# Two projections whose first call takes four column blocks, and eleven products at the start

## The chip, the cores and the metric

The kernel runs on one core of a Trainium2 chip. Its engines each work through their own row of instructions in order: TensorE (PE in the profile, with PEld for the loading of weights), VectorE (DVE), ScalarE (ACT), GpSimd (POOL), and SyncE (SP), which here issues the transfers. The metric is the device time of one execution in microseconds (us).

## The reference

One layer of an encoder: 256 rows of x, 2048 wide, 256 rows of memory. The parts that the change touches are the two projections `w_out` and `w_o`, each added to x. The attention's weights are a softmax over the memory rows for each of four heads.

```python
h = rms_norm(x, norm_mix_g[l])
x = x + hybrid_mixer(h, ...)            # ends in: merged @ w_out
h = rms_norm(x, norm_x_g[l])
mem_n = rms_norm(mem, norm_mem_g[l])
x = x + cross_attention(h, mem_n, w_xq[l], w_xkv[l], w_xo[l])
...
def cross_attention(h, mem_n, w_q, w_kv, w_o):
    q = (h @ w_q).reshape(b, s, XATTN_HEADS, XATTN_DH)
    k, v = jnp.split(mem_n @ w_kv, 2, axis=-1)
...
    p = jax.nn.softmax(scores, axis=-1)
    o = jnp.einsum("bhsm,bmhd->bshd", p, v).reshape(b, s, D_MODEL)
    return o @ w_o
```

Behind these stands an MLP with 8192 hidden columns. All inputs are float32.

## The kernel before

Every large product streams a weight matrix from memory once. `fetch` (L74 to L98) brings 1 MB of it at a time into a buffer `raw` of which there are three, and splits it in two halves: for each half ACT writes the high part `whi` (L93) and DVE the rest `wlo` (L94), in three buffers each. With `rush` the 1 MB comes in two transfers of 512 KB. A product of two float32 matrices is then made of two or three products of such parts. The activations lie as such pairs too, in tiles named `q` (`Quad`).

The order of the instructions on each engine comes from a scheduler that goes by the order of the code, by data that must be there, by free buffers and by priorities; `tc.high_priority(offset=...)` moves what stands in it forward. Each engine then keeps its row and waits at each instruction until its inputs and its buffer are there.

PSUM, where TensorE writes, is given out from three rings: `s0` and `s1`, two banks each, by `stream_ps()`, and `b`, four banks, by `bank()`. The ring `b` serves the transposes in `to_feature` (L238), the attention's scores (`sps`), its transposed weights (`tps`), its outputs (`ops`), and more.

There are two ways to stream a matrix. `chunk` (L134 to L136) makes 512 columns for 2 row tiles at a time, three products each. `blocks` (L158 to L180) makes `nb` blocks of 128 columns: for each of the 16 row blocks `nb` products with `whi` (L172, 512 wide) and `nb` with `wlo` (L174, 256 wide). One fetch holds 16 / `nb` row blocks. At the end ACT (L178) and DVE (L179) take each block out of its bank into a tile `bo`, of which there are two, and `evac` goes on with it.

Three places matter here.

The start: the first `chunk` is that of the values (`w_xkv`, `values(0)`). Its `before` loads 512 columns of the memory rows (`xc`, `load_mem`), transposes them on TensorE against `ident` (L238), and ACT (L251) and DVE (L252) write them into `q`, scaled by `gains`. ACT also sums squares of those rows (`junk`, L266). `ident` is made by POOL at L207, and the gains come through a transpose of 16 rows (`grow`, L224).

`w_out`: the last `chunk` of the mixer's gates (`w_in`, columns from `C_TB`) ends in `evac` of `sig_gate` (ACT L802 writes `gth`, DVE L814 and L816 write `yg`), then `to_feature` transposes `yg` into the last quad of `merged`. The call `residual_pass(merged, w_out[0], G_X, "n2", load_x)` follows: eight calls of `blocks` with two column blocks each, each with its 256 columns of x through `loader`.

`w_xo`: for each head the attention makes the scores (L104 to L106, 24 products into `sps`), their maximum (DVE L929, L930), the exponentials (ACT L934), the scaled weights `pr` (DVE L936, L938), four transposes of these into `tps` (L943), their parts `pth` and `ptl` (ACT L100, DVE L101), and the outputs (L104 to L106 again, from `pth`, `ptl`, `vvh`, `vvl`). After the last head comes `residual_pass(att, w_xo[0], G_FFN, "n3")`, which needs all heads for its 16 row blocks but takes the first twelve from the earlier heads. The scheduler lays products of it between the instructions of the last head.

Of the kernel before, what the change touches and what calls it, by code (L numbers as in the profile page):

```python
# [17 lines left out]
P = 128  # L18
# [32 lines left out]
def trunk(ctx: ExitStack, tc: tile.TileContext, x, mem, positions, norm_mix_g, w_in, conv_w, gdn_a_log, gdn_dt_bias,  # L51
# [4 lines left out]
    act, vec, pool, pe = nc.scalar, nc.vector, nc.gpsimd, nc.tensor  # L56
# [9 lines left out]
    def stream_ps():  # L66
        s0 = psp.tile([P, 512], F32, name="s0", tag="s0", bufs=2)
        s1 = psp.tile([P, 512], F32, name="s1", tag="s1", bufs=2)
        return s0, s1

    def bank():
        return psp.tile([P, 512], F32, name="b", tag="b", bufs=4)


    def fetch(pieces, k, n, rush=False, hold=None, at=0):

        raw = wp.tile([P, k * n], F32, name="raw", tag="raw", bufs=3)
        rv = raw.rearrange("p (k n) -> p k n", k=k)
        with tc.high_priority(offset=100000):
            for off, ap in pieces:  # L80
                src = ap.rearrange("(k p) n -> p k n", p=P)
                for ks in ((slice(0, k // 2), slice(k // 2, k)) if rush else (slice(0, k),)):
                    nc.sync.dma_start(rv[:, ks, off:off + ap.shape[1]], src[:, ks, :])
            got = []
            for i in range(2):
                if hold:
                    both = hold().both
                    hi, lo = (both[:, a:a + 2, :].rearrange("p a s -> p (a s)") for a in (0, 2))
                else:
                    hi, lo = (wp.tile([P, 1024 + ROOM], F32R, name=e, tag=e, bufs=3)[:, at:at + k * n // 2]  # L90
                              for e in ("whi", "wlo"))
                src = raw[:, i * k * n // 2:(i + 1) * k * n // 2]
                act.activation(hi, src, AF.Copy)  # L93
                vec.tensor_sub(lo, src, hi.bitcast(F32))  # L94
                got.append((hi.rearrange("p (k n) -> p k n", n=n), lo.rearrange("p (k n) -> p k n", n=n)))
        return got
# [61 lines left out]
    def blocks(quads, w, c0, nb, evac):  # L158

        k = 16 // nb
        ps = stream_ps()
        n = nb * P
        for g in range(KT // k):
            halves = fetch([(0, w[g * k * P:(g + 1) * k * P, c0:c0 + n])], k, n, at=SHIFT)
            for i in range(k):
                kk = g * k + i
                xh, xhl = quads[kk // 4][0][:, kk % 4, :], quads[kk // 4].both[:, kk % 4, :]
                wh, wl = (a[:, i % (k // 2), :] for a in halves[i // (k // 2)])  # L170
                for b in range(nb):
                    pe.matmul(ps[b], wh[:, b * P:(b + 1) * P], xhl, start=kk == 0, stop=False)  # L172
                for b in range(nb):
                    pe.matmul(ps[b][:, :S], wl[:, b * P:(b + 1) * P], xh, start=False, stop=kk == KT - 1)  # L174
        for b in range(nb):
            with tc.high_priority(offset=50000):
                o = sm.tile([P, S], F32, name="bo", tag="bo", bufs=2)
                act.activation(o, ps[b][:, S:], AF.Copy)  # L178
                vec.tensor_add(o, o, ps[b][:, :S])  # L179
                evac(b, o)  # L180
# [23 lines left out]
    ident = cp.tile([P, P], F32, name="ident")  # L204
# [7 lines left out]

    def rsqrt(o, i):
        pool.tensor_tensor(o, i, nhalf_pow[:, :o.shape[1]], op=ALU.pow)

    gains = cp.tile([P, 64], F32, name="gains")

# [37 lines left out]
    def rms_cols(name, ssq, count=D):  # L255

        s = sm.tile([P, NT], F32, name=f"{name}_s", tag="rc_s")
        vec.tensor_reduce(s, ssq, axis=AX.X, op=ALU.add)
        vec.tensor_scalar(s, s, 1.0 / count, EPS, op0=ALU.mult, op1=ALU.add)
        r = cp.tile([P, NT], F32, name=f"{name}_r")  # L260
        rsqrt(r, s)
        return r
# [67 lines left out]
    for k2 in range(8):  # L330
        ps = bank()
# [9 lines left out]
        for f in range(2):  # L341
            k = 2 * k2 + f
# [13 lines left out]
    for a in range(2):  # L356
        ps = bank()
# [156 lines left out]
    for b2 in range(8):  # L514
        ko = kv.tile([P, 2, S], F32, name="ko", tag="vo", bufs=2)

        def evac_k(b, ps):
            vec.tensor_mul(ko[:, b, :], ps, mrow)

        blocks(memq, w_xkv[0], b2 * 256, 2, evac_k)  # L520
        nc.sync.dma_start(kt_d[:, 2 * b2:2 * b2 + 2, :], ko)
        for h in ((0,), (2, 4), (6, 8), (10,), (12,), (14,), (), ())[b2]:
            decays(h)
        if 2 <= b2 < 6:
            ret_decays(2 * b2 - 4)
# [24 lines left out]
    def gdn_stream(grp):  # L550
# [4 lines left out]
        for pr in range(2):  # L555
# [5 lines left out]
            for part, c0, bofs in ((1, C_GQ, 0), (0, C_GK, 16), (2, C_GV, 32)):  # L561
                def evac(b, ps, part=part, bofs=bofs):
                    if part < 2:
                        conv_silu(bofs + h0 + b, ps, kq[:, b, part, :])
                    else:
                        vt = mx.tile([P, S], F32, name="vt", tag="vt", bufs=2)
                        conv_silu(bofs + h0 + b, ps, vt)
                        vts.append(vt)
                blocks(h1, w_in[0], c0 + h0 * GD, 2, evac)
# [169 lines left out]
    def retention(j, yr):  # L739
        qk = mx.tile([P, 4, S], F32, name="qk", tag="qk", bufs=1)  # L740

        for a2, c0 in ((0, C_RQ), (2, C_RK)):
            def evac_qk(b, ps):

                rb = mx.tile([P, S], F32, name="rb", tag="rb", bufs=2)
                act.activation(rb[0:64], ps[64:128], AF.Copy)
                act.activation(rb[64:128], ps[0:64], AF.Copy)
                o = qk[:, a2 + b, :]
                vec.tensor_mul(o, ps, cos)
                vec.tensor_mul(rb, rb, sin)  # L750
                vec.tensor_add(o, o, rb)

            blocks(h1, w_in[0], c0 + 256 * j, 2, evac_qk)
# [104 lines left out]
    rt = tp.tile([P, KT, S], F32, name="rt", tag="rt", bufs=1)  # L858
# [3 lines left out]
    def quad_b():  # L862
        return new_quad(q2p, 4)
# [8 lines left out]
    def residual_pass(quads, w, gain, name, loader=None):  # L872
        nxt = []
        acc = xa.tile([P, S], F32, name="acc2", tag="acc2", bufs=2)
        vec.memset(acc, 0.0)
        for b2 in range(8):
            xc = loader(b2) if loader else None
            if b2 % 2 == 0:
                nxt.append(quad_b())

            def evac(b, ps):
                k = 2 * b2 + b
                vec.tensor_add(rt[:, k, :], ps, xc[:, b, :] if loader else rt[:, k, :])
                g = gains[:, gain + k:gain + k + 1]
                qh, ql = (a[:, k % 4, :] for a in nxt[-1])
                act.activation(qh, rt[:, k, :], AF.Copy, scale=g)
                vec.scalar_tensor_tensor(ql, rt[:, k, :], g, qh.bitcast(F32), op0=ALU.mult, op1=ALU.subtract)
                sq = xa.tile([P, S], F32, name="sq2", tag="sq2", bufs=2)
                act.activation(sq, rt[:, k, :], AF.Square)
                vec.tensor_add(acc, acc, sq)  # L890

            blocks(quads, w, b2 * 256, 2, evac)
        ps = bank()
        for t in range(NT):
            pe.matmul(ps[:, 2 * t:2 * t + 2], acc[:, t * P:(t + 1) * P], ones[:, :2], start=True, stop=True)
        s = sm.tile([P, NT], F32, name=f"{name}_s", tag="rc_s")
        vec.tensor_scalar(s, ps[:, 0:4:2], 1.0 / D, EPS, op0=ALU.mult, op1=ALU.add)
        r = cp.tile([P, NT], F32, name=f"{name}_r")
        rsqrt(r, s)
        return nxt, r  # L900

    def load_x(b2):
        xc = xa.tile([P, 2, S], F32, name="xc2", tag="xc2", bufs=2)
        nc.sync.dma_start(xc, xt_d[:, 2 * b2:2 * b2 + 2, :])
        return xc

    h2, rstd2 = residual_pass(merged, w_out[0], G_X, "n2", load_x)
    rstd2s = cp.tile([P, NT], F32, name="rstd2s")
    vec.tensor_scalar_mul(rstd2s, rstd2, XD ** -0.5)
# [3 lines left out]
    for h in range(XH):  # L913
# [14 lines left out]
        nb = xa.tile([P, NT], F32, name="nb", tag="nb", bufs=2)  # L928
# [27 lines left out]
        att.append(quad)  # L956

    h3, rstd3 = residual_pass(att, w_xo[0], G_FFN, "n3")
    rstd3q = cp.tile([P, NT], F32, name="rstd3q")
    vec.tensor_mul(rstd3q, rstd3, rstd3)  # L960
# [7 lines left out]
    for c in range(4):  # L968
        for t in range(NT):
            ps = bank()  # L970
# [95 lines left out]
```

## Time and profile before

| | |
|---|---|
| runs | 2086.66, 2086.51 and 2084.16 us; median 2086.51 us |
| the profiled execution | 2084.37 us |
| its span in the profile | 2082.6 us |
| instructions in the trace | 28439 |
| mean granted clock of TensorE | 0.999 |
| bytes moved | 405.09 MB, 195 GB/s |

The span runs from the first to the last event of the execution; 1.8 us lie around it. In the lists below a line has a start, a duration, the engine, the line of the kernel, the operation, what it writes and reads, how many instructions are put together in it, and in brackets how long the engine had been idle before and what ended that. PE's durations overlap, since products are pipelined: the distance of two starts is what one costs.

### The profile page before, as it was taken

To read this page: it belongs to the slowest core of one execution; us is meant where nothing else is said; L and a number is where in the kernel's file an instruction comes from. 1 tells how busy PE (TensorE), PEld (TensorE's weight loads), DVE (VectorE), ACT (ScalarE), POOL (GpSimd) and SP (SyncE) were. 2 spreads that over 40 slices of the span, in tenths; PEclk is the share of its full clock that TensorE was granted. 3 is DMA by queue.
4 is the path that set the end of the run, shared out by engine and by line. 5 is a ranking of instruction groups with operands and counts; after the bars stand their busy time and mean duration, and the time that the engine had idled before them with its cause. 6 is when DMAs were issued, how large, how long until landed. Compare 5 with 4: busy or idle time off the path is not lost.

```text
span 2082.6 us, 28439 instructions
## 1 busy us (share of the span) xinstructions
PE 2062.4 (99%) x11028; PEld 1776.8 (85%) x11028; DVE 1396.9 (67%) x2261; ACT 1081.8 (52%) x1630; POOL 31.1 (1%) x37
## 2 busy tenths in 40 slices
PE   8999999999999999999999999999999999999998
PEld 6888888888888888888888898888888888888887
DVE  6785779577966786678757665756556546645654
ACT  7554564566446644565455555554444434434444
POOL 0000000000000000000000000000000000000000
PEclk9999999999999999999999999999999999999999
DMA  8796656555555565555657654666566556556653
GB/s 292 234 315 224 202 175 211 168 182 175 199 185 165 175 200 186 171 183 172 199 183 235 193 182 142 188 196 196 189 196 188 195 189 194 190 196 188 195 189 142
DMA packets 314342, 405.09 MB, mean 195 GB/s; under 512 B 18512, under 2 KB 222304, under 8 KB 314080
## 3 DMA queue, kind: packets, MB, share of 16 engines
q1 hardware_dynamic: 314208, 403.29, 59.8%
q8 instruction: 86, 1.41, 0.3%
q14 instruction: 48, 0.39, 0.1%
HBM read 389.61 MB, written 13.65 MB: 194 GB/s over the span
## 4 chain that ended last, share of the span: by engine, by line
PE 97%; DMA 1%; SPq 1%; DVE 0%; issue 0%; ACT 0%; ACTq 0%; POOLq 0%; POOL 0%; DVEq 0%
PE s L172 34%; PE s L174 17%; PE s L135 14%; PE s L136 14%; PE s L134 14%; PE b L684 1%; PE b L587 1%; DMA xc<-x 1%; PE b L104 0%; PE b L106 0%; PE b L105 0%; SPq L285 0%; DMA vr<-vv_d 0%; PE b L589 0%; PE b L585 0%
## 5 line engine op out<-in xcount | busy, mean ns | idle before, releaser
L94 DVE TENSOR_TENSOR wlo<-raw,whi 128x1024 fp32r<-128x1024 f32 x700 | 855.4, 1223 | 575.4 <-ACT whi L93 571.7
L93 ACT ACTIVATE whi<-raw 128x1024 fp32r<-128x1024 f32 x700 | 741.4, 1060 | 814.9 <-PE s L172 378.9
L172 PE MATMUL s<-q,whi 128*128 128x512 f32 x3072 | 959.9, 393 | 3.4 <-DVE bo L179 3.2
L174 PEld LDWEIGHTS s<-q,wlo 128*128 128x128 f32 x3072 | 575.2, 188 | 123.2 <-DVE wlo L94 1.1
L174 PE MATMUL s<-q,wlo 128*128 128x256 f32 x3072 | 615.8, 280 | 0.5 <-DVE wlo L94 0.5
L135 PE MATMUL s<-wlo,q 128*128 128x512 f32 x1264 | 495.7, 392 | 0.5 <-DVE wlo L94 0.5
L136 PE MATMUL s<-whi,q 128*128 128x512 f32 x1264 | 491.8, 390 | 0.0
L172 PEld LDWEIGHTS s<-q,whi 128*128 128x128 f32 x3072 | 468.8, 188 | 7.3 <-DVE bo L179 3.6
L134 PE MATMUL s<-whi,q 128*128 128x512 f32 x1264 | 452.3, 390 | 0.0
L134 PEld LDWEIGHTS s<-whi,q 128*128 128x128 f32 x1264 | 237.7, 188 | 48.9 <-ACT q L251 0.4
L135 PEld LDWEIGHTS s<-wlo,q 128*128 128x128 f32 x1264 | 237.8, 188 | 48.3 <-DVE wlo L94 0.9
L136 PEld LDWEIGHTS s<-whi,q 128*128 128x128 f32 x1264 | 237.7, 188 | 47.4
L179 DVE TENSOR_TENSOR bo<-bo,s 128x256 f32<-128x256 f32 x192 | 72.2, 413 | 0.0
L178 ACT ACTIVATE bo<-s 128x256 f32<-128x256 f32 x192 | 62.4, 372 | 17.3 <-DVE dj L593 17.3
L536 DVE SCALAR_TENSOR_TENSOR acc<-bo,cw,acc 128x255 f32<-128x255 f32 (+2 forms) x144 | 61.8, 477 | 3.0 <-ACT acc L533 2.8
L644 DVE TENSOR_TENSOR pr<-lw,tw 32x31 f32<-32x31 f32 (+15 forms) x124 | 40.3, 325 | 10.5 <-DMA lw<-scr_l 8.7
L646 DVE TENSOR_TENSOR tw<-tw,pr 32x31 f32<-32x31 f32 (+15 forms) x124 | 40.6, 327 | 2.1
L994 DVE SCALAR_TENSOR_TENSOR res<-s,rstd3q,res 128x512 f32<-128x512 f32 (+1 forms) x32 | 22.3, 735 | 12.0 <-PE s L136 12.0
L986 DVE TENSOR_TENSOR q<-hs,q 128x256 fp32r<-128x256 f32 x64 | 24.1, 419 | 0.8 <-ACT q L985 0.8
L983 DVE SCALAR_TENSOR_TENSOR hs<-bo 128x256 f32<-128x256 f32 x64 | 24.2, 419 | 0.0
L533 ACT ACTIVATE acc<-bo,cw 128x256 f32<-128x256 f32 x48 | 22.0, 499 | 1.6 <-PE b L585 0.8
L985 ACT ACTIVATE q<-hs 128x256 fp32r<-128x256 f32 x64 | 22.7, 402 | 0.0
(313 smaller groups left out, 1041.7 us busy)
## 6 DMA issues: line engine op xcount, KB each, us to landing
raw<-w_in SPq DMA_DIRECT2D x143, 1024.0 KB, 4.9
raw<-w_ff SPq DMA_DIRECT2D x128, 1024.0 KB, 5.2
raw<-w_xkv SPq DMA_DIRECT2D x31, 1024.0 KB, 5.7
raw<-w_out SPq DMA_DIRECT2D x16, 1024.0 KB, 5.3
raw<-w_xq SPq DMA_DIRECT2D x16, 1024.0 KB, 6.1
raw<-w_xo SPq DMA_DIRECT2D x16, 1024.0 KB, 5.8
dec_d<-dec_w SPq DMA_DIRECT2D x8, 384.0 KB, 11.1
dec<-dec_d SPq DMA_DIRECT2D x8, 384.0 KB, 4.3
```

Source lines behind the costliest of these rows:

```text
L93: act.activation(hi, src, AF.Copy)
L94: vec.tensor_sub(lo, src, hi.bitcast(F32))
L134: pe.matmul(o, xh, wh, start=first, stop=False)
L135: pe.matmul(o, xh, wl, start=False, stop=False)
L136: pe.matmul(o, xl, wh, start=False, stop=last)
L172: pe.matmul(ps[b], wh[:, b * P:(b + 1) * P], xhl, start=kk == 0, stop=False)
L174: pe.matmul(ps[b][:, :S], wl[:, b * P:(b + 1) * P], xh, start=False, stop=kk == KT - 1)
L178: act.activation(o, ps[b][:, S:], AF.Copy)
L179: vec.tensor_add(o, o, ps[b][:, :S])
L536: vec.scalar_tensor_tensor(acc[:, d:], ps[:, :S - d], cw[:, j, blk:blk + 1], acc[:, d:], op0=ALU.mult, op1=ALU.add)
L644: vec.tensor_mul(pv, lw[:, j, j + 1:32].unsqueeze(2).to_broadcast([32, n, j + 1]), tw[:, j, 0:j + 1].unsqueeze(1).to_broadcast([32, n, j + ...
L646: vec.tensor_sub(tw[:, j + 1:32, 0:j + 1], tw[:, j + 1:32, 0:j + 1], pv)
```

## The change

The first call of each residual projection takes 512 columns, four blocks, where it was two calls of 256; the other six stay. The two further banks come from the ring `b`. In that call a fetch holds 4 row blocks of 512 columns instead of 8 of 256; the number of products, fetches and transfers is the same, and two tiles of x are loaded ahead of the call. At the start eleven products `ident` by `ident` are written into a bank of the ring `b`, at the highest priority in the program; nobody reads them. Lines behind the change have numbers 5 or 6 higher.

```diff
         k = 16 // nb
-        ps = stream_ps()
+        ps = stream_ps() if nb < 3 else (*stream_ps(), bank(), bank())
...
+    with tc.high_priority(offset=300000):
+        wps = bank()
+        for _ in range(11):
+            pe.matmul(wps[:, :P], ident, ident, start=True, stop=True)
...
-        for b2 in range(8):
-            xc = loader(b2) if loader else None
+        for b2 in (0, 2, 3, 4, 5, 6, 7):
+            nb = 2 if b2 else 4
+            xc = [loader(b2 + i) for i in range(nb // 2)] if loader else None
...
-                vec.tensor_add(rt[:, k, :], ps, xc[:, b, :] if loader else rt[:, k, :])
+                vec.tensor_add(rt[:, k, :], ps, xc[b // 2][:, b % 2, :] if loader else rt[:, k, :])
...
-            blocks(quads, w, b2 * 256, 2, evac)
+            blocks(quads, w, b2 * 256, nb, evac)
```

The order of the instructions differs at three places only: up to the end of the first values, around the first call of `w_out`, and around the first call of `w_xo`. Everything between and behind them stands in the same order as before.

At the start ACT's row, before the change, is this one (the first `whi` is the first half of the first 1 MB, the second `whi` its other half; `xc` are memory rows, `b` their transposes):

```order
L203 ACTIVATE warm<-warm 128x1
L93 ACTIVATE whi<-raw 128x1024
L266 ACTIVATE junk,ssqm<-xc 128x512 x2
L251 ACTIVATE q<-b,gains 128x256
L93 ACTIVATE whi<-raw 128x1024
L251 ACTIVATE q<-b,gains 128x256 x2
```

And with the change:

```order
L203 ACTIVATE warm<-warm 128x1
L93 ACTIVATE whi<-raw 128x1024 x2
L271 ACTIVATE junk,ssqm<-xc 128x512
L256 ACTIVATE q<-b,gains 128x256 x2
L271 ACTIVATE junk,ssqm<-xc 128x512
L256 ACTIVATE q<-b,gains 128x256
```

Both halves of the first piece now stand ahead of the first `q`, and one sum of squares instead of two.

On PE at `w_out`, before the change, the transposes of `yg` stand behind all 24 pairs of products of the first twelve row blocks for the first two column blocks, and one pair of L172 of the next call (here the end of these and the beginning of that call):

```order
L174 MATMUL s_10101<-q,wlo 128x256
L174 MATMUL s_10102<-q,wlo 128x256
L172 MATMUL s_10207<-q,whi 128x512
L172 MATMUL s_10208<-q,whi 128x512
L238 MATMUL b<-ident,yg 128x128 x2
L174 MATMUL s_10207<-q,wlo 128x256
L174 MATMUL s_10208<-q,wlo 128x256
L172 MATMUL s_10207<-q,whi 128x512
```

And with the change, where the four column blocks are `s_10115`, `s_10116` and two banks `b`:

```order
L172 MATMUL s_10115<-q,whi 128x512
L172 MATMUL s_10116<-q,whi 128x512
L174 MATMUL s_10115<-q,wlo 128x256
L174 MATMUL s_10116<-q,wlo 128x256
L243 MATMUL b<-ident,yg 128x128 x2
L172 MATMUL b<-q,whi 128x512 x2
L174 MATMUL b<-q,wlo 128x256 x2
L172 MATMUL b<-q,whi 128x512 x2
L174 MATMUL b<-q,wlo 128x256 x2
```

The first two transposes now stand behind the 12 pairs of six row blocks, and ahead of the 12 pairs that the same row blocks have on the two banks `b`; the other six transposes follow those.

On PE at `w_xo`, before the change, thirty products of the projection stand between the last head's scores and the transposes of its weights. These are the last of them:

```order
L172 MATMUL s_12190<-q,whi 128x512
L172 MATMUL s_12191<-q,whi 128x512
L174 MATMUL s_12190<-q,wlo 128x256
L174 MATMUL s_12191<-q,wlo 128x256
L943 MATMUL b<-ident,pr 128x128 x4
L172 MATMUL s_12190<-q,whi 128x512
L172 MATMUL s_12191<-q,whi 128x512
```

With the change the scores' last products, the transposes and the first products from `pth` stand side by side, and behind them six row blocks on one bank `b`:

```order
L104 MATMUL b<-kth,qth 128x256
L105 MATMUL b<-ktl,qth 128x256
L106 MATMUL b<-kth,qtl 128x256
L949 MATMUL b<-ident,pr 128x128 x4
L104 MATMUL b<-pth,vvh 128x256 x2
L172 MATMUL b<-q,whi 128x512
L174 MATMUL b<-q,wlo 128x256
L172 MATMUL b<-q,whi 128x512
L174 MATMUL b<-q,wlo 128x256
```

The two blocks on `s0` and `s1` have gone ahead of the scores by six row blocks, as far as the three buffers of `whi` reach, and the two blocks on `b` come where the banks of scores and weights come free.

## The prediction

> **What bounds the kernel now.** I read the page's busy times and its chain first, then the list of what PE waits for, then the timeline at the places that the change touches.
>
> ```profile
> PE 2062.4 (99%) x11028; PEld 1776.8 (85%) x11028; DVE 1396.9 (67%) x2261; ACT 1081.8 (52%) x1630; POOL 31.1 (1%) x37
> ...
> PE 97%; DMA 1%; SPq 1%; DVE 0%; issue 0%; ACT 0%; ACTq 0%; POOLq 0%; POOL 0%; DVEq 0%
> ```
>
> PE is busy for 99% of the span and carries 97% of the chain. So a change that leaves the products as they are can gain only what PE now waits or works at a slow pace, and it loses whatever new waits it makes. All waits of PE are these (what, for whom, us in total, times, longest):
>
> ```profile
> PE b L238 <- DMA xc<-mem: 5.1, 1, 5.1
> PE s L172 <- DVE bo L179: 3.2, 2, 2.1
> PE b L224 <- DMA grow<-norm_mem_g: 2.5, 1, 2.5
> PE s L135 <- DVE wlo L94: 0.5, 1, 0.5
> PE s L174 <- DVE wlo L94: 0.5, 1, 0.5
> ```
>
> The second line is what four column blocks can remove: twice PE waits for a bank until DVE has taken out the blocks of the calls before, 2.1 us at `w_out` and 3.2 − 2.1 = 1.1 us at `w_xo`. The first line stands ahead of the first products; its transfer isn't touched.
>
> PE has two paces. These are its first rows, and two from later:
>
> ```profile
> 7.89 1.97 PE L238 MATMUL b<-ident,xc 128*128 128x128 f32 x8 [5.14 <-DMA xc<-mem]
> ...
> 9.85 0.80 PE L134 MATMUL s<-whi,q 128*128 128x512 f32 x1
> ...
> 10.44 0.63 PE L135 MATMUL s<-wlo,q 128*128 128x512 f32 x1
> ...
> 10.87 0.63 PE L134 MATMUL s<-whi,q 128*128 128x512 f32 x1
> ...
> 11.29 0.57 PE L135 MATMUL s<-wlo,q 128*128 128x512 f32 x1
> ...
> 12.15 0.39 PE L134 MATMUL s<-whi,q 128*128 128x512 f32 x1
> ...
> 29.20 0.39 PE L136 MATMUL s<-whi,q 128*128 128x512 f32 x1
> ...
> 29.43 0.39 PE L135 MATMUL s<-wlo,q 128*128 128x512 f32 x1
> ```
>
> From start to start a 512-wide product costs 0.43 us at first (10.44 to 10.87) and 0.23 us later (29.20 to 29.43). The change of pace lies between 11.29 and 12.15, some 3.8 us after steady work began at 7.89. Warming PE up thus costs about 3.8 × (1 − 0.23 / 0.43) = 1.8 us of lost work at most; I call 1.6 the price of being cold once, and use it three times below. That PE also cools down shows at the end, in the table by stretches (PE busy, then the others, the granted clock third from last):
>
> ```profile
> 1095.40:1097.60 2.20, 0.12 (x2) 0.01 (x1) 2.20 (x4) 1.84 (x4) 0.00 (x0) 1.00 0.75 228
> ...
> 2074.40:2076.70 2.30, 0.02 (x1) 0.00 (x0) 1.50 (x5) 0.43 (x1) 0.56 (x1) 1.00 0.73 281
> 2076.70:2080.00 3.30, 0.00 (x0) 0.00 (x0) 0.72 (x2) 0.91 (x2) 0.00 (x0) 0.50 0.68 261
> ```
>
> After 2.3 us without a product the clock is at half. The pause of 2.1 us at `w_out` (first row) left it at 1.00. So the point from which a pause cools PE lies near 2.2 us, and whether pauses of 2 to 3 us appear decides this prediction as much as their length.
>
> **The change part by part: the start.** Eleven float32 products of 128 by 128 are added. The eight transposes of that size above take 1.97 us cold; a float32 product against float32 weights runs in two passes here, which I estimate at 11 × 2 × 0.22 = 4.8 us cold, half of that warm. They begin when `ident` is there, near 1.5 us, and end by 6.3, before the memory rows come at 7.89. So they cost nothing themselves; without that cover they would cost their 2.4 to 4.8 us. But the first `q` moves on ACT:
>
> ```profile
> 8.71 0.63 ACT L266 ACTIVATE junk<-xc 128x512 f32<-128x512 f32 x1
> ...
> 9.34 0.45 ACT L251 ACTIVATE q<-b,gains 128x256 fp32r<-128x256 f32 x1
> 9.70 1.04 ACT L93 ACTIVATE whi<-raw 128x1024 fp32r<-128x1024 f32 x1
> ...
> raw<-w_xkv SPq DMA_DIRECT2D x1, 512.0 KB, 6.9
> ```
>
> The second half of the first piece is issued at 2.2 and lands 6.9 us later, at 9.1 (last line, a list of transfers). Before, ACT made the first `q` at 9.34, ahead of that half's `whi`; now `whi` stands first, so ACT waits to 9.1, works 1.06, sums squares (0.75 to the next start, as from 7.96 to 8.71), and makes `q` from about 10.95 to 11.4. The first L134 moves from 9.85 to 11.45. If PE were warm there, it would win back the cold products, (11.7 − 9.85) × (1 − 0.23 / 0.43) = 0.9 us, and 0.5 us of a wait that ends at a fixed time:
>
> ```profile
> 31.00 0.50 PE L135 MATMUL s<-wlo,q 128*128 128x512 f32 x1 [0.50 <-DVE wlo L94]
> ```
>
> 1.6 − 0.9 − 0.5 is +0.2; with one further short wait for the other `q` I take **+0.4 us**. But between the products and the first L134 PE works only for the transposes, 1 to 2 us out of more than 5. By the pauses above it comes to its first rows cold, and they cost **+1.6** more. Ends of this part: −0.5 (the order on ACT hurts less) to +2.5.
>
> **`w_out`.** The wait of 2.1 goes: the third call finds `s0` and `s1` free, as the four blocks of the first hold two banks `b` besides. Its eight evacuations (ACT and DVE, 0.4 us each) then lie beside the next products. In exchange PE meets the transposes of `yg` sooner:
>
> ```profile
> 1072.28 0.39 PE L172 MATMUL s<-q,whi 128*128 128x512 f32 x1
> ...
> 1076.59 0.60 ACT L802 ACTIVATE gth<-s 128x512 f32<-128x512 f32 x1 [0.38 <-DVE yg L808]
> ...
> 1077.61 0.69 DVE L814 SCALAR_TENSOR_TENSOR yg<-gth,yg 128x512 f32<-128x512 f32 x1
> 1078.33 0.69 DVE L816 TENSOR_TENSOR yg<-yg,yr 128x512 f32<-128x512 f32 x1
> ```
>
> PE starts the projection at 1072.28. Only 12 pairs of products now stand ahead of the transposes, 12 × 0.345 = 4.1 us (0.345 from the rows at `w_xo` below), so PE is there at 1076.4. `gth` is ready at 1077.2, then L814 and L816 take 0.69 each, so `yg` is ready at 1078.6 if DVE goes straight on. The new wait is 2.2 us; behind it in PE's row stand the 12 pairs on the two banks `b`, which need no `yg` and can't pass. It takes the place of the 2.1: **−0.1 us**, ends −2.1 (no new wait) and +0.5 (a `wlo` between L814 and L816). Whether 2.2 us cools PE is open; if so, +1.6. The transfers for x, two at once now, are issued with nothing waiting on them until the first evacuation.
>
> **`w_xo`.** Removed: the wait of 1.1, and 0.3 between 1294.16 and 1294.59, which a 256-wide product fills with 0.12 only. Added: between the last scores and the transposes PE has nothing in its row. Before, it had thirty products there:
>
> ```profile
> 1280.21 0.28 PE L106 MATMUL b<-kth,qtl 128*128 128x256 f32 x1
> ...
> 1280.53 0.69 DVE L929 TENSOR_REDUCE nb<-b 128x2 f32<-128x512 f32 x1 [0.46 <-PE b L106]
> ...
> 1281.26 0.16 DVE L930 SCALAR_TENSOR_TENSOR nb<-nb,rstd2s 128x2 f32<-128x2 f32 x1
> ...
> 1281.52 0.56 ACT L934 ACTIVATE pr<-b,nb,rstd2s 128x256 f32<-128x256 f32 x1 [2.70 <-DVE nb L930]
> ...
> 1282.07 0.55 ACT L934 ACTIVATE pr<-b,nb,rstd2s 128x256 f32<-128x256 f32 x1
> ...
> 1282.95 0.62 DVE L938 TENSOR_SCALAR pr<-pr,sums 128x256 f32<-128x256 f32 x2
> ...
> 1284.01 0.62 PE L172 MATMUL s<-q,whi 128*128 128x512 f32 x2
> ...
> 1284.70 0.62 PE L172 MATMUL s<-q,whi 128*128 128x512 f32 x2
> ...
> 1285.40 0.60 PE L943 MATMUL b<-ident,pr 128*128 128x128 f32 x4
> ...
> 1286.37 0.58 ACT L100 ACTIVATE pth<-b 128x512 fp32r<-128x512 f32 x1
> ...
> 1294.16 0.28 PE L106 MATMUL b<-pth,vvl 128*128 128x256 f32 x1
> ...
> 1294.59 0.73 PE L172 MATMUL s<-q,whi 128*128 128x512 f32 x2
> ```
>
> From the end of the scores (1280.49) to the scaled weights (1282.95 + 0.62 = 1283.57) maximum, exponential and scaling take 3.1 us, and none of it depends on PE. (1284.01 to 1284.70 gives 0.69 for two pairs.) Now PE stands still for these 3.1 us, does the transposes, stands again until `pth` is there, 0.58 and two hand-overs or about 0.75, and waits another 0.15 for a `wlo` whose buffer came free late. That is 4.0 us for 1.4 removed: I take **+2.5 us**; ends +1.0 (if the scheduler's earlier rows let ACT or DVE run ahead) and +3.5. A pause of 3.1 us is longer than the 2.3 that halved the clock, so another **+1.6**.
>
> The sum is 0.4 + 1.6 − 0.1 + 2.5 + 1.6 = **+6.0 us**. The profiled execution took 2084.37 us (span 2082.6), 2.1 below the median of the runs shown and near their lowest; the mean of all four is 2085.4. I count from that mean: 2091.4, say 2091. [...]
>
> **The rivals.** (A, the forecast) PE is cold at its first rows and after the softmax of the last head: +6.0; 4.4 if one of the two stays warm. (B) PE stays warm through all pauses, so that only the waits count: 0.4 − 0.1 + 2.5 = +2.8, 2088, no measurable change. The place is the 3.1 us ahead of L949; it decides from the pause that cools PE, and if that is longer than 3.1 us with some work around it, B holds. For it: 2.1 us did no harm at `w_out`. Against it: the end of the span, 2.3 us. [...] (C) All old waits go and the new ones don't come, because ACT and DVE, less held up, hand over sooner: −1.4 − 2.1 at the projections and −1.4 at the start gives −4.9 us, 2080.5. Against it stand the rows of the order: the 3.1 us hold five dependent steps, none with a wait for a busy engine. (D) As A, and the 2.2 us at `w_out` cools PE too: +7.6, 2093. That the products don't do what they seem made for, first rows at full pace, is part of A and D; alone it is worth 1.6.
>
> **How the numbers follow.** A 0.48, D 0.15, B 0.27, C 0.10. About 0.2%, or 4.2 us, is what a measurement of this kernel can tell from no change. D, and A but for its smaller sizes (0.08), are slower; B is mostly the same (0.05 slower); C is mostly faster (0.09). So slower 0.60, same 0.31, faster 0.09. The range leaves out most of C and the far end of D: from 2085.5 (B with the wait at `w_out` gone too, 2086.1, and some of another term's lower end, since all lower ends hardly come together) to 2096 (D with its terms at their upper ends, +2.1, or 2095.1, and the spread of runs).
>
> **What would show it.** Right: the first L134 near 11.4 with a pitch of 0.43; a wait of about 2.2 us of L243 for `yg` and 3.1 us of L949 for `pr`; no wait of L172 for `bo` at either projection; a granted clock under 1 behind L949. Wrong: a first L134 before 10.5, or L949 without a wait; a pitch of 0.23 at 11.5 and a clock of 1.00 behind the softmax give B.

## The result, and the profile after

The changed kernel took 2091.87 us (median of 7 runs, 2088.86 to 2093.35), the kernel before 2084.26 us in runs beside it (7 runs, 2083.18 to 2086.66). The ratio is 1.0031 with a 95% interval from 1.0021 to 1.0041, so it is slower by about 6.5 us. (The ratio goes by the means, 2091.3 and 2084.9 us; the medians lie 7.6 us apart.) The forecast was 2091 us and slower. The profiled execution of the changed kernel has a span of 2090.1 us, 7.5 us longer than that of before.

The page's busy times and its chain read as before; PE is still the bound:

```profile
PE 2071.0 (99%) x11050; PEld 1783.7 (85%) x11050; DVE 1397.8 (67%) x2261; ACT 1081.5 (52%) x1630; POOL 30.0 (1%) x37
...
PE 98%; DVE 0%; DMA 0%; ACT 0%; issue 0%; SPq 0%; ACTq 0%; POOLq 0%; POOL 0%
```

PE is busy for 8.6 us more with only 22 instructions more, of which the products at the start account for 5.1. So a part of the loss is not waiting but slow work. The list of what PE waits for has new names (what, for whom, us in total, times, longest):

```profile
PE b L949 <- DVE pr L944: 3.0, 1, 3.0
PE s L134 <- ACT q L256: 2.2, 1, 2.2
PE b L243 <- DVE yg L821: 2.2, 1, 2.2
PE b L219 <- POOL ident L207: 1.5, 1, 1.5
PE b L243 <- DMA xc<-mem: 0.9, 1, 0.9
PE b L104 <- ACT pth L100: 0.7, 1, 0.7
PE s L174 <- DVE wlo L94: 0.5, 1, 0.5
```

Both waits of L172 for a bank are gone. In their place stand a wait for `yg` at `w_out`, and two for the softmax at `w_xo` (for `pr` and for `pth`); and the first L134 waits for `q`.

Where the 7.5 us come from is read from rows that both programs have:

| row | before | after | later by | the stage's share |
|---|---|---|---|---|
| transposes of `g_rows` (L437, behind the start) | 95.93 | 98.05 | 2.12 | start +2.12 |
| first L172 of `w_out` | 1072.28 | 1074.24 | 1.96 | between −0.16 |
| transposes of the last head but one (L943) | 1258.48 | 1261.91 | 3.43 | `w_out` +1.47 |
| first transposes behind `w_xo` (L972) | 1378.50 | 1386.08 | 7.58 | `w_xo` +4.15 |
| end of the span | 2082.6 | 2090.1 | 7.5 | rest −0.1 |

The experiments below are read by the same five rows. Between the start and `w_out`, where the order is the same in all of them, single executions differed from that of before by −0.3 to +1.1 us. At the start the two executions without products differed from it by −0.1 and −0.5. So a stage's share is good to about half a us and that long stretch to about one.

The pace of PE in the timeline, at the start and behind the two new pauses:

```profile
1.53 5.06 PE L219 MATMUL b<-ident 128*128 128x128 f32 x22 [1.53 <-POOL ident L207]
...
7.61 1.09 PE L243 MATMUL b<-ident,xc 128*128 128x128 f32 x8 [0.85 <-DMA xc<-mem]
10.91 0.80 PE L134 MATMUL s<-whi,q 128*128 128x512 f32 x1 [2.21 <-ACT q L256]
11.51 0.63 PE L135 MATMUL s<-wlo,q 128*128 128x512 f32 x1
11.93 0.63 PE L134 MATMUL s<-whi,q 128*128 128x512 f32 x1
...
1080.75 0.41 PE L243 MATMUL b<-ident,yg 128*128 128x128 f32 x2 [2.17 <-DVE yg L821]
...
1285.06 0.72 PE L949 MATMUL b<-ident,pr 128*128 128x128 f32 x4 [2.96 <-DVE pr L944]
1286.46 0.75 PE L104 MATMUL b<-pth,vvh 128*128 128x256 f32 x2 [0.69 <-ACT pth L100]
```

The eight transposes (L243) took 1.09 us here, at a granted clock of 1.00, against 1.97 us before: the products had warmed PE. But then it waits 2.21 us for `q`, and starts its first rows at 0.42 us from start to start (11.51 to 11.93), cold. The table by stretches of the same kernel (granted clock third from last) shows how long PE is cold each time:

```profile
10.90:16.80 5.90, 5.89 (x14) 4.63 (x15) 3.14 (x6) 3.59 (x9) 0.00 (x0) 0.50 1.05 407
16.80:20.00 3.20, 3.20 (x20) 2.73 (x19) 2.15 (x3) 2.70 (x7) 0.00 (x0) 1.00 1.05 408
1079.00:1083.00 4.00, 2.25 (x11) 2.01 (x12) 2.71 (x4) 1.01 (x3) 0.00 (x0) 0.84 0.00 0
1083.00:1087.00 4.00, 4.00 (x20) 3.44 (x20) 1.83 (x2) 2.17 (x3) 0.00 (x0) 0.73 0.17 31
1284.00:1287.50 3.50, 1.76 (x8) 1.39 (x9) 1.47 (x4) 0.92 (x3) 0.00 (x0) 0.86 0.00 0
1287.50:1291.00 3.50, 3.50 (x17) 3.08 (x16) 0.00 (x0) 0.00 (x0) 0.00 (x0) 0.65 0.00 0
2085.00:2086.00 1.00, 0.00 (x0) 0.00 (x0) 0.00 (x0) 0.14 (x1) 0.00 (x0) 0.63 0.62 240
```

The first two rows read 0.50 and 1.00. Taken as one of these two at every moment, the clock has a mean of 0.84 over 4 us if it is at half for 0.16 × 2 × 4 = 1.28 us. So it fell at 1081.72 and rose at 1083 + 0.27 × 2 × 4 = 1085.16: 3.44 us at half. At `w_xo` it fell at 1286.52 and rose at 1289.95, 3.43 us. At the start it stayed at half for the whole 5.9 us.

### The profile page after: what moved, and what is told of

It reads as the page before. It is cut to its first block, busy times and chain, and to the rows that moved or that the text cites. A ratio compares the mean times of both kernels' runs of the same rounds, so it can differ in the third digit from the quotient of the medians.

```text
span 2090.1 us, 28485 instructions
## 1 busy us (share of the span) xinstructions
PE 2071.0 (99%) x11050; PEld 1783.7 (85%) x11050; DVE 1397.8 (67%) x2261; ACT 1081.5 (52%) x1630; POOL 30.0 (1%) x37
## 4 chain that ended last, share of the span: by engine, by line
PE 98%; DVE 0%; DMA 0%; ACT 0%; issue 0%; SPq 0%; ACTq 0%; POOLq 0%; POOL 0%
PE s L172 33%; PE s L174 17%; PE s L135 14%; PE s L134 14%; PE s L136 14%; PE b L689 1%; PE b L172 1%; PE b L592 1%; PE b L104 1%; PE b L106 1%; PE b L105 1%; PE b L174 0%; DMA raw<-w_xkv 0%; PE b L243 0%; PE b L594 0%
## 5 line engine op out<-in xcount | busy, mean ns | idle before, releaser
L172 PE MATMUL s<-q,whi 128*128 128x512 f32 x3008 | 937.8, 393 | 0.0
L174 PEld LDWEIGHTS s<-q,wlo 128*128 128x128 f32 x3008 | 563.1, 188 | 122.9 <-DVE wlo L94 1.4
L174 PE MATMUL s<-q,wlo 128*128 128x256 f32 x3008 | 598.8, 279 | 0.5 <-DVE wlo L94 0.5
L172 PEld LDWEIGHTS s<-q,whi 128*128 128x128 f32 x3008 | 457.5, 188 | 1.8
L134 PE MATMUL s<-whi,q 128*128 128x512 f32 x1264 | 452.2, 390 | 2.2 <-ACT q L256 2.2
L134 PEld LDWEIGHTS s<-whi,q 128*128 128x128 f32 x1264 | 237.9, 188 | 51.1 <-ACT q L256 2.4
L807 ACT ACTIVATE gth<-s 128x512 f32<-128x512 f32 x32 | 19.0, 594 | 9.6 <-DVE yg L813 4.2
L172 PE MATMUL b<-q,whi 128*128 128x512 f32 x64 | 23.1, 433 | 0.0
```

The source lines that it names most:

```text
L134: pe.matmul(o, xh, wh, start=first, stop=False)
```

## The experiments

The theory: the change costs what the new waits are longer than the old ones, and 1.6 us more each time that a pause of 2 to 3 us cools PE; at the start, the products move `q` behind a `whi` on ACT. The rivals: the waits alone; the products themselves; three buffers of `whi`, not the banks, as the reason for the pauses. All ratios are against runs of the kernel before on the same chip.

**Only the products.**

```diff
+    with tc.high_priority(offset=300000):
+        wps = bank()
+        for _ in range(11):
+            pe.matmul(wps[:, :P], ident, ident, start=True, stop=True)
```

> Only the eleven products, both projections as before. If the start's loss comes from the order on ACT and a cold PE: first L134 near 10.9 us with 0.43 us from start to start until about 15 to 17 us, then everything as before; about +2.0 us against before, so a ratio near 1.001. If the products do what they seem made for: first L134 by 9.9 us at 0.23 us, and about -1.4 us. If they only cost nothing: no difference at all in the first 31 us.

Measured: ratio 1.0005 (0.9996 to 1.0015), no difference that can be told, where about +2.0 us had been expected. The trace shows the start much as expected: first L134 at 10.85 us, 0.43 us from start to start, and +0.89 us for the start, still +0.82 at the first L172 of `w_out`. The transposes took 1.97 us, so here eleven products hadn't warmed PE. At the last head but one nothing of the loss is left (−0.05 us). From this kernel's list of waits:

```profile
PE s L172 <- DVE bo L179: 2.4, 2, 1.2
```

The old wait for a bank at `w_out` is still there in this kernel, and it is 1.2 us instead of 2.1. It ended at 1097.59 us before and at 1097.55 here: ACT and DVE take the blocks out behind keys and values that a transfer brings (before, ACT waits 1.14 us for `kr` and 0.70 us for `vr` there), so PE's late arrival shortens it. In the changed kernel that wait is gone, and a late start stays late. The profiled execution is the fastest of its ten (2084.25 to 2088.06 us); where the others spend more wasn't traced.

**Only the four column blocks** (the change without the lines above).

> Only the four column blocks at both projections, no products at the start. Waits and clock together: the first 31 us as before, +1.5 us at w_out (a wait of 2.2 us for yg in place of 2.1 us for a bank, and 1.6 us of half pace where the pause cools PE), +4.4 us at w_xo (pauses of 3.0 and 0.7 us for 1.4 us of old waits, and 1.6 us of half pace): about +5.9 us, ratio near 1.0028. Waits alone, with the clock untouched: +2.4 us, ratio near 1.0012. If the start alone were the cause: no change.

Measured: 2089.95 against 2084.8 us, ratio 1.0023 (1.0014 to 1.0032). By stages −0.13 us at the start, which is that of before in its order, +0.99 between (0.8 of it are two longer waits of PE for a `wlo`, at 124 and 1027 us), +1.46 at `w_out` and +5.33 at `w_xo`. This profiled execution, 2092.17 us, is the slowest of its ten. Waits alone would have given +2.4 us. `w_xo` costs 1.2 us more than in the changed kernel, at the same waits of 3.0 and 0.7 us. The stretches behind its softmax:

```profile
1284.00:1287.50 3.50, 2.81 (x11) 2.32 (x12) 0.75 (x2) 0.60 (x1) 0.00 (x0) 0.59 0.02 5
1287.50:1291.00 3.50, 3.50 (x14) 3.11 (x14) 0.00 (x0) 0.00 (x0) 0.00 (x0) 0.50 0.00 0
1291.00:1294.00 3.00, 3.00 (x23) 2.92 (x22) 0.70 (x2) 1.20 (x2) 0.00 (x0) 0.93 0.00 0
```

PE was at half for 2.87 + 3.50 + 0.42 = 6.8 us here, twice as long as in the changed kernel. What a pause costs is thus not one number, though the program is the same at this place.

**The pause filled.** Work for PE in the softmax of the last head, which can't run before the maxima:

```diff
         vec.scalar_tensor_tensor(nb, nb, -1.0, rstd2s, op0=ALU.mult, op1=ALU.mult)
+        tps = bank()
+        if h == XH - 1:
+            pe.matmul(tps[:, :2], ident, nb, start=True, stop=True)
+            for _ in range(8):
+                pe.matmul(tps[:, :P], ident, ident, start=True, stop=True)
...
-        tps = bank()
```

> The changed kernel, with nine products into the bank of the transposes between the last head's scores and these transposes: one that reads the negated maxima (so that it can't run before them) and eight of ident by ident, about 1.8 us of work in a pause of 3.0 us. The wait for the weights ends at the same time. If the half pace behind the softmax comes from the pause: granted clock 1.00 behind L953, 0.23 us from start to start, and about 1.6 us less than the changed kernel at w_xo (+2.8 instead of +4.4 us there). If the half pace comes from something else: the same +4.4 us as without the nine.

Measured: ratio 1.0020 (1.0010 to 1.0029), an interval that overlaps with that of the changed kernel, so what the filling does is read from the stage. `w_xo` costs +2.68 us, 1.47 less than in the changed kernel. Rows and stretches of this kernel there:

```profile
1282.61 2.03 PE L941 MATMUL b<-ident 128*128 128x128 f32 x16
1284.48 0.60 PE L953 MATMUL b<-ident,pr 128*128 128x128 f32 x4
...
1285.00:1288.00 3.00, 2.31 (x14) 2.02 (x14) 0.69 (x1) 0.60 (x1) 0.00 (x0) 1.00 0.00 0
1288.00:1291.00 3.00, 3.00 (x26) 2.95 (x25) 0.65 (x1) 0.60 (x1) 0.00 (x0) 1.00 0.00 0
```

More work in the same place made the stage faster, and the clock stays at 1.00. So the half pace comes from the pause, and the waits alone are worth the other 2.7 us, as far as one execution shows.

**Other banks.** The two further blocks from the rings `s0` and `s1`:

```diff
-        ps = stream_ps() if nb < 3 else (*stream_ps(), bank(), bank())
+        ps = stream_ps() if nb < 3 else (*stream_ps(), *stream_ps())
```

> The changed kernel, with the two further banks taken from the rings s0 and s1 instead of b. If sharing the ring b with scores and weights is what leaves PE without products during the softmax: no wait of L949 for pr and none of L243 for yg, clock 1.00 at both projections; instead the third call has to wait for a bank until the first blocks are taken out, 1 to 3 us each time: about +2 us against before in all (the start's +2.0, and -1 to +2 at the projections). If the pauses come from the three buffers of whi alone, whatever the banks: L949 waits about 3 us as in the changed kernel, and the time is that of the changed kernel or more.

Measured: 2090.89 against 2084.8 us, ratio 1.0027 (1.0016 to 1.0037), more than expected. Its waits:

```profile
PE s L172 <- DVE bo L179: 4.7, 2, 2.4
...
PE s L172 <- ACT gth L807: 0.6, 1, 0.6
```

Both new pauses are gone: with a free ring `b` the scheduler lays products into the softmax again. So the shared ring made them, not the three buffers. But now all four `s` banks belong to the first call, and the next call's first product waits for the evacuation, 2.41 us at `w_out` and 2.29 at `w_xo`. At `w_xo` that is +1.22 us, within what was expected, and the clock stays at 1.00 (1303 to 1309 us). At `w_out` it is +2.82, since this pause cools PE (0.50 from 1102 to 1104 us, start to start 0.43). The estimate had left that out. So of two pauses of nearly one length in one execution one cooled PE and the other didn't:

```profile
1100.31 0.51 PE L172 MATMUL s<-q,whi 128*128 128x512 f32 x1 [2.41 <-DVE bo L179]
1102.00:1104.00 2.00, 2.00 (x8) 1.71 (x8) 2.00 (x7) 1.78 (x6) 0.00 (x0) 0.50 1.09 388
1307.00 0.50 PE L172 MATMUL s<-q,whi 128*128 128x512 f32 x1 [2.29 <-DVE bo L179]
1303.00:1309.00 6.00, 3.71 (x22) 3.11 (x22) 4.29 (x9) 2.90 (x8) 0.00 (x0) 1.00 0.57 175
```

**Other banks, and the evacuation begun earlier.** No products at the start. In the last fetch of a four-block call the row blocks are done column block by column block, so that the first block is whole earlier:

```diff
+            sets = [range(nb)] if nb < 3 or (g + 1) * k < KT else [(b,) for b in range(nb)]
+            for cols_now in sets:
...
-                for b in range(nb):
+                    for b in cols_now:
```

> Four column blocks with all banks from the rings s0 and s1, no products at the start, and the last fetch of the four-block call done column block by column block in each half, so that the first block is whole about 2.1 us before the call ends and its bank can be taken out beside the other blocks' products. If what is left of the loss with s banks is the wait for the evacuation: no wait of L174 for bo over 0.5 us at either projection, no pause that cools PE, -2.1 us at w_out and -1.2 us at w_xo against before, about -3 us in all (ratio near 0.9985). If ACT's wait for the keys and values of the first head holds the evacuation whatever the order: 1 to 2 us of wait remain at w_out and only w_xo gains, about -1 us.

Measured: 2083.08 against 2085.05 us, ratio 0.9991 (0.9982 to 1.0000). PE waits for no evacuation (`bo`) any more:

```profile
PE b L240 <- DMA xc<-mem: 4.8, 1, 4.8
PE b L226 <- DMA grow<-norm_mem_g: 2.4, 1, 2.4
PE s L174 <- ACT gth L804: 0.6, 1, 0.6
PE s L176 <- DVE wlo L94: 0.5, 1, 0.5
PE s L135 <- DVE wlo L94: 0.4, 1, 0.4
```

By stages −1.03 us at `w_out` and −1.24 at `w_xo`. At `w_out` 2.1 had been expected; 0.6 of the difference is the wait for a bank that the last gate's `gth` is read from, new with four `s` banks (third line); the rest wasn't traced.

**Eight products**, projections as before (`range(8)` for `range(11)` in the first experiment).

> Eight products instead of eleven, both projections as before. With eight the order on ACT is that of before: the first q ahead of the second half's whi. If the eleven cost their time through that order: first L134 back at 9.6 to 9.9 us, and no loss at the start (0 +/- 0.5 us; PE is cold or warm there by where the clock's change falls, since eight products end near 5 us and leave 2.5 us of pause). If the products cost time themselves, or any product ahead of the transposes does: +0.5 to +2 us.

Measured: ratio 0.9996 (0.9987 to 1.0005). First L134 at 9.23 us, so the order on ACT is what had moved it. But the start still costs +0.43 us in this execution:

```profile
7.60:8.90 1.30, 0.76 (x7) 0.53 (x5) 0.00 (x0) 1.27 (x5) 0.00 (x0) 0.75 1.02 377
8.90:11.00 2.10, 1.77 (x4) 1.48 (x5) 1.33 (x2) 1.95 (x4) 0.00 (x0) 0.50 1.03 394
```

PE was warm for the transposes and fell to half at 8.25 us, after its 2.0 us of pause ahead of them. Being early did not pay since the rows were done cold.

**The pause before the first rows filled**, in the changed kernel:

```diff
                 to_feature(lambda t, f: xc[:, t, f * P:(f + 1) * P], G_MEM + 4 * c, memq[c])
+                if c == 0:
+                    for _ in range(9):
+                        pe.matmul(wps[:, :P], xc[:, 0, :P], ident, start=True, stop=True)
```

> The changed kernel with nine more products between the first transposes and the first L134, each of a piece of the memory rows by ident, so that they can't run before these rows are there: about 2 us of work (4 if cold) in the pause of 2.2 us before the first L134. The order on ACT stays that of the changed kernel. If the start's loss is the order on ACT and a cold PE, about half each: first L134 still near 10.9 us, now with 0.23 us from start to start from the first or second microsecond on, and the start costs 0.3 to 0.8 us against before instead of 1.2 to 2.0. If PE is cold there for another reason: a pitch of 0.43 us for 3 us or more as in the changed kernel, and no gain or a loss.

Measured: ratio 1.0018 (1.0008 to 1.0028), about 2.7 us less than the changed kernel has against its own runs of before, though the two intervals overlap. The start costs −0.09 us, against +0.9 to +2.1 in the four executions with the eleven products alone ahead of it:

```profile
8.54 2.17 PE L310 MATMUL b<-ident,xc 128*128 128x128 f32 x18
11.36 0.50 PE L134 MATMUL s<-whi,q 128*128 128x512 f32 x1 [0.65 <-ACT q L256]
11.70 0.40 PE L135 MATMUL s<-wlo,q 128*128 128x512 f32 x1
11.94 0.39 PE L134 MATMUL s<-whi,q 128*128 128x512 f32 x1
```

The first L134 comes 1.5 us later than in the kernel before, and yet PE is through the start no later, at 0.23 us from start to start from the beginning. In this execution warmth is worth more than the order on ACT. With `w_out` at +1.47 and `w_xo` at +4.02 us the rest of the changed kernel's loss stays.

**Put together.** The banks and the evacuation of the experiment with the earlier evacuation, with eleven products and the nine of the one above:

> The four-block calls with s banks and the last fetch done column block by column block (w_out -1.0, w_xo -1.2 us in the run without products), with eleven products and nine more before the first L134 at the start (-0.4 us there). If the stages add up: about -2.5 us against before, ratio near 0.9988, no pause of PE over 1 us behind 11.4 us. If the start interferes with the projections: less.

Measured: 2081.39 against 2085.24 us, ratio 0.9980 (0.9971 to 0.9989). By stages −0.56 at the start, −0.21 between, −1.39 at `w_out` and −1.24 at `w_xo`, −3.4 in all. This version beats both kernels. That the products give the gain at the start isn't shown: the experiment with the same banks and evacuation, without any, has −0.47 there. The two profiled executions, 1.8 us apart, differ most in the stretch between (+1.13 and −0.21), where the order is the same.

**The same with eight and four.**

> The same with eight products, which leaves the order on ACT as before, and four more before the first L134. First L134 by 9.5 us. If the clock holds over the pause from 5 to 7.3 us: 0.23 us from start to start by 10 us, -1.5 us at the start, -3.5 us in all (ratio near 0.9983). If it falls there, as it did in the run with eight products alone: about 0 at the start, -2.2 us in all.

Measured: ratio 0.9989 (0.9980 to 0.9997). PE was cold: the transposes took 1.97 us, the four products 1.9 us instead of 0.9, and so the first L134 came at 10.87 us, not by 9.5, with 0.43 us from start to start until about 13.3. No row shows that the eight products had warmed it before. The start costs +0.46, the projections −0.61 and −1.22 us.

## Why the prediction was right

- *The start*, forecast at 0.4 + 1.6 = 2.0, measured 2.12 in the changed kernel's profiled execution, but 0.89, 0.90 and 1.14 in three experiments with the same start. The forecast size is thus the upper end, and how long PE stays cold there (5.9 us or 3.4) makes most of the difference: 2.5 us more at half are about 1.2 us. The first L134 was placed at 11.45 and came at 10.91, as the second half landed at 8.8 instead of 9.1. It was cold as forecast, for 5.9 us here instead of 3.8; in the experiment with the filled softmax pause for 0.42 × 2 × 4 = 3.4 us (clock 0.58 from 12 to 16 us), where the start cost 0.90. The step's two causes are shown apart, each in one profiled execution: eight products, with the old order on ACT, bring the first L134 to 9.23, and nine more products ahead of it bring the share to −0.09.
- *`w_out`*, forecast at −0.1, with 1.6 more if 2.2 us of pause cools PE, which was left open. The wait for `yg` is 2.17 and PE cooled: +1.47. So it was the case called D, 7.6 us in all, that came in the profiled execution, with 7.5. The forecast's own case stopped short by this term. Behind it stands a reading that failed: that there is a length, near 2.2 us, from which a pause cools PE. With eight products a pause of 1.97 us cooled PE; in the experiment with other banks 2.41 us did and 2.29 didn't. So its length alone doesn't decide; what else does isn't shown.
- *`w_xo`*, forecast at 2.5 + 1.6 = 4.1, measured 4.15. The wait of 3.1 was 2.96, that of 0.75 was 0.69. The filled pause shows the two terms alone: 2.68 and 1.47. The price of 1.6 us was taken from 3.8 us at the start; it fits one stretch of 3.4 us at half, 3.4 × (1 − 0.23 / 0.43) = 1.6, and would have been too small for the 6.8 us of the second experiment.
- *Case B*, PE stays warm through all pauses, falls with the granted clock behind the pauses (0.50 for 3.44 us at `w_out` and 3.43 us at `w_xo`) and with the filled ones. Its condition, that only a pause longer than 3.1 us cools PE, doesn't hold here: single pauses of 2.17 and 2.41 us were enough.
- *Case C*, no new waits, falls with the list of waits.
- The forecast took the terms to add up. In the changed kernel they do. With the old wait at `w_out` they don't: the products alone come 0.82 us late to it and get that back there.
- The total came out closer than its parts. As measured in the profiled executions they are 2.12 + 1.47 + 4.15 = 7.7, less 0.2 elsewhere; the forecast lacked 1.6 of that at `w_out`. But it counted from the mean of all executions before, and the means differ by 6.4 us. That 6.0 lies so near to 6.4 is in part luck.

The runs spread from 2088.86 to 2093.35 us, and the granted clock that is on record for each goes with the time: 0.997 for 2088.86 and 2089.00 us, 0.996 for the four from 2091.36 to 2092.51, 0.995 for 2093.35. With the clock again taken as 1.00 or 0.50, a thousandth of 2085 us is half pace for 0.001 × 2 × 2085 = 4.2 us. So the same kernel is cold for longer in some executions than in others. The kernel before is, too: of the 21 runs of it beside the experiment with the earlier evacuation 13 have a clock of 0.999, with a mean of 2084.59 us, and 8 have 0.998, with 2086.29. Its profiled execution is at half only at the start (0.43 us from start to start until about 11.7 us) and behind the last products (a clock of 0.50 from 2076.7 us on), which helps to explain why the profiled executions lie further apart (7.5 us) than the means. Where PE was cold in the others wasn't traced.

## What to carry to other kernels

When a change of banks or blocks removes a wait, read in the new order what the engine finds in its row behind the next dependent chain: a filler that has moved ahead leaves the chain bare. On a kernel that keeps TensorE at 99% a pause of 2 us can be paid twice, as a pause and as half pace behind it, at one place and not at another: here pauses of 1.97, 2.17 and 2.41 us had half pace behind them, and pauses of 2.08 and 2.29 us hadn't. So products whose result nobody reads can pay inside a pause (1.47 us at `w_xo`); products that ended 2 us before the work began didn't (the start cost 0.43 us). Judge such a change by many runs, and single profiles by their clock. A delay can vanish in a later wait that ends at a fixed time, as the 0.82 us at `w_out` did; removing that wait brings it back.

## What the runs showed of the hardware

Behind some pauses of PE the granted clock fell to 0.50, behind others it stayed at 1.00:

| execution | pause of PE | us | granted clock |
|---|---|---|---|
| eight products | ahead of the first transposes | 1.97 | at half from 8.25 us |
| before | first wait for `bo`, `w_out` | 2.08 | 1.00 up to 1103 us |
| changed kernel | `yg`, `w_out` | 2.17 | at half from 1081.72 to 1085.16 us |
| changed kernel | `q`, start | 2.21 | at half from 9.96 to 16.8 us |
| other banks | `bo`, `w_xo` | 2.29 | 1.00 from 1303 to 1309 us |
| other banks | `bo`, `w_out` | 2.41 | 0.50 from 1102 to 1104 us |
| changed kernel | `pr`, `w_xo` | 2.96 | at half from 1286.52 to 1289.95 us |

The length of the pause doesn't part these seven: 2.08 and 2.29 us left the clock at 1.00, while 1.97, 2.17 and 2.21 us did not.

Nor did the clock fall at one distance from a pause. In the changed kernel the pause at `w_out` ended at 1080.75, and the clock fell 0.97 us later, with PE at work again. At `w_xo` the pause for `pr` ended at 1285.06 and the clock fell 1.46 us later, just behind the wait of 0.69 us for `pth` that ended at 1286.46. At the start the transposes ended at 8.70, and the clock fell 1.26 us into the pause behind them, at 9.96. Behind the last product of the kernel before it fell after 2.3 us, at 2076.7.

The stretches at half were not of one length either: 3.44 us at `w_out` and 3.43 us at `w_xo` in the changed kernel, 3.4 us at the start of the experiment with the filled softmax pause, but 6.8 us at the start of the changed kernel (PE worked in 5.9 of them) and 6.8 us at `w_xo` in the second experiment, there behind the same pauses of 3.0 and 0.7 us.

What sets these moments and lengths isn't shown: no experiment varied by itself when a pause begins, or how much PE works around it.
